# Both score blocks of a tile multiplied before the first read, and PSUM tiles of one bank for the paired products

## The chip, the cores and the metric

The kernel runs on one core of one Trainium2 chip. The metric is the device time of one execution in microseconds, the median of the runs shown. The engines are TensorE (PE; its weight loads are listed apart as PEld), VectorE (DVE), ScalarE (ACT), GpSimd (POOL) and SyncE (SP, which here issues most transfers).

## The reference

One inference step of a hybrid decoder layer, for a prompt of 512 tokens and for 8 decode sequences of 4 tokens (544 token columns in all, width 2048), all in float32:

```python
u = x @ w_in                      # 18952 columns: q, k, v, o, z of the mLSTM; q, k, v, z of attention; two merge gates; i, f
h_m, C, n, m = mlstm(q_m, k_m, v_m, ig, lf, C0, n0, m0)
h_a = sliding-window attention with sinks (32 heads of 64, 4 KV heads, window 128)
br_m = layernorm_per_head(h_m) * norm_w * sigmoid(o_m) * silu(z_m)
br_a = h_a * silu(z_a)
y = sigmoid(g_m) * (br_m @ w_proj_m) + sigmoid(g_a) * (br_a @ w_proj_a)
out = layernorm(alpha * x + y @ w_out) * ln_w + ln_b
```

The prompt's attention goes by blocks of 128 queries; block j sees the keys of blocks j-1 and j:

```python
s = q @ k.T / sqrt(64) - slope * dist       # masked outside the window
p = softmax(concat([s, sink]))[:-1]
out = p @ v
```

Further outputs are the states and the last keys and values of both parts.

## The kernel before

Every float32 product is made of three products of a faster type: the weights are split into a high part `wh` (ScalarE, line 184) and a low part `wl` (VectorE, line 185), the activations likewise, and hi*hi, hi*lo and lo*hi are added up in PSUM.

The work has three stretches. First come x, its transposes and a few plain products for keys, values and gates (to about 87 us). Then the stage of this change, 72 *pairs* (`paired`, lines 627 to 651): a pair takes two column tiles of 128 of `w_in` and computes a 2 x 2 block product (two halves of the inner dimension, two halves of the 544 columns) in seven products in place of eight, with sums of the halves. Last come `w_proj_a`, `w_proj_m` and `w_out` as plain products (from about 1988 us).

A pair runs as seven steps n = 0 to 6. `half_product` (line 582) issues 24 matmuls of 272 columns: 16 with `wh` (line 593), 8 with `wl` (line 595). They go to three sums, called bank 0 (A), 1 (D) and 2 (B), in the order `BANK = [0, 1, 2, 0, 2, 1, 2]`. Products 0, 1 and 2 open a sum, the later ones add to it. After each product `gather` (line 597) reads the sum that was just written:

- n = 0: ScalarE copies A to `p1` (line 604); n = 1: ScalarE copies D (line 612); n = 3: ScalarE copies A (line 617)
- n = 2, 4, 5, 6: VectorE combines B, B, D and B with earlier results (lines 615, 619, 621, 623)

The sums lie in PSUM tiles of two banks from the pool `psA`, which has two buffers: X is allocated at n = 0 and holds A and D in its two banks; Y is allocated at n = 2 and uses only its first bank, for B. The same pool serves the plain products. A second pool, `psB`, has four tiles of one bank (`sm()`) for everything else.

The weights of step n + 2 are split ahead (`prepare`, with a higher priority), into two buffers each for `wh` and `wl`. The weights of the next pair are loaded at n = 3 and n = 4.

Between the steps `tick()` lets other generators issue a piece of their work. One of them, `attentions()`, goes through 16 attentions of two heads each (lines 682 to 745). Its first part makes the scores: for each head and each of four blocks j, two matmuls (`k1`, `k2`, line 700) and one VectorE instruction (line 702) that adds the distance term, clips and keeps the row minimum. Blocks 0 and 1 lie in the two halves of one `sm()` tile, blocks 2 and 3 in those of another. The exponentials follow on ScalarE (line 711), the normalisation (line 717), two steps later the transposes (line 728) and the product with the values (line 738). The attentions take place from about 193 to 1070 us; after them comes the attention of the decode tokens and then, from about 1190 us, their mLSTM part (lines 1042 to 1089).

The order of TensorE's instructions in this stage is that of the program text (`manual_schedule`, line 1183). The other engines' queues are ordered by a planner from priorities; all waits between engines are set from the tiles that an instruction reads and writes.

Of the kernel before, what the change touches and what calls it, by code (L numbers as in the profile page):

```python
# [15 lines left out]
F32 = mybir.dt.float32  # L16
F32R = mybir.dt.float32r
AF = mybir.ActivationFunctionType
ALU = mybir.AluOpType
# [54 lines left out]
def _build(tc, nc, i, o, es):  # L74
    PSUM = bass.MemoryType.PSUM
    ALL = slice(0, 128)

    def pool(stack, name, bufs, space=None, side=None):
        kw = {"space": space} if space is not None else {}
        if space is None:  # L80
            kw["side"] = side or "right"
            kw["reuse_waits"] = "tile"
        return stack.enter_context(tc.tile_pool(name=name, bufs=bufs, **kw))

    y_p, y_s, C_p, n_p, m_p, kb_p, vb_p, C_s, n_s, m_s, kb_s, vb_s = o
    V, A, G, PE = nc.vector, nc.scalar, nc.gpsimd, nc.tensor
# [3 lines left out]
    wr = pool(es, "wr", 3)  # L90
    wp = pool(es, "wp", 2)
    evp = pool(es, "ev", 3)
    psA = pool(es, "psA", 2, PSUM)
    psB = pool(es, "psB", 4, PSUM)
    dr = pool(es, "dr", 1, bass.MemoryType.DRAM)

    count = [0]

    def nm(s):
        count[0] += 1  # L100
        return f"{s}_{count[0]}"

    def sm():
        return psB.tile([128, 512], F32, tag="sm", name=nm("sm"))
# [16 lines left out]
    def spawn(g):  # L121
        live.append(g)
# [8 lines left out]
    def drain():  # L131
        while live:
            tick()
# [10 lines left out]
    nsinkb = cst.tile([128, AH], F32, name="nsinkb")  # L144
# [53 lines left out]
    EVEN = ((0, 0, 272), (1, 272, 272))  # L198

    def mm():  # L200
        return psA.tile([128, 2, 512], F32, tag="mm", name=nm("mm"))

    def gemm(wv, c0, xh, xl, cols=EVEN, raws=(None, None), every=8, prio=0, before=None):
        ps = mm()
# [31 lines left out]
    HT = T // 2  # L236
# [277 lines left out]
    for kk in range(2):  # L514
        ps = gemm(win, VA_ + kk * 128, xh, xl, raws=((raw0[0], raw0[1]), (raw0[2], None))[kk], every=4, prio=150 * kk,
                  before=gates_between if kk else None)
# [63 lines left out]
            add("b21", "b21", "b11")  # L580

    def half_product(w, n):
        bank = BANK[n]
        if n == 0:
            w["X"] = mm()
        if n == 2:
            w["Y"] = mm()
        ps = w["Y"][:, 0, :HT] if bank == 2 else w["X"][:, bank, :HT]
        wh, wl = w.pop(("hl", n))
        x, first = XS[n], n in (0, 1, 2)  # L590
        for k in range(8):
            for p in range(2):
                PE.matmul(ps, wh[:, k], x(p, k), start=(first and k == 0 and p == 0), stop=False, skip_group_check=True)  # L593
        for k in range(8):
            PE.matmul(ps, wl[:, k], x(0, k), start=False, stop=(k == 7), skip_group_check=True)  # L595

    def gather(w, n):

        A0, D0, B0 = w["X"][:, 0, :HT], w["X"][:, 1, :HT], w.get("Y")
        B0 = B0[:, 0, :HT] if B0 is not None else None  # L600
        sc = w["scale"]
        if n == 0:
            w["p1"] = pe_.tile([128, HT], F32, tag="p1", name=nm("p1"))
            A.activation(w["p1"][:], A0, AF.Copy, scale=sc)  # L604
            return
        if n == 1:
            w["O1"], w["O2"] = ev(), ev()
        c11, c21 = (w["O1"][:, c:c + HT] for c in (0, HT))
        c12, c22 = (w["O2"][:, c:c + HT] for c in (0, HT))
        p1 = w["p1"][:]  # L610
        if n == 1:
            A.activation(c11, D0, AF.Copy, scale=sc)  # L612
            G.tensor_tensor(out=c22, in0=p1, in1=c11, op=ALU.subtract)  # L613
        elif n == 2:
            V.scalar_tensor_tensor(c12, B0, sc, p1, op0=ALU.mult, op1=ALU.subtract)
        elif n == 3:
            A.activation(c11, A0, AF.Copy, scale=sc)  # L617
        elif n == 4:
            V.scalar_tensor_tensor(c22, B0, -sc, c22, op0=ALU.mult, op1=ALU.add)
        elif n == 5:  # L620
            V.scalar_tensor_tensor(c12, D0, sc, c12, op0=ALU.mult, op1=ALU.add)
        else:
            V.scalar_tensor_tensor(c21, B0, sc, p1, op0=ALU.mult, op1=ALU.subtract)
# [3 lines left out]
    def paired(work, first=iter(())):  # L627

        steps = [(w, n) for w in work for n in range(7)]
        ready = 0  # L630
        load_a(work[0])
        load_b(work[0])
        for at, (w, n) in enumerate(steps):

            while ready < min(at + 3, len(steps)):
                with tc.high_priority(offset=AHEAD):
                    prepare(*steps[ready])
                ready += 1
            p = at // 7 + 1
            if p < len(work):  # L640
                if n == 3:
                    load_a(work[p])
                elif n == 4:
                    load_b(work[p])
            half_product(w, n)
            with tc.high_priority(offset=AHEAD):
                gather(w, n)
            next(first, None)
            if n == 6:
                w["end"](w["O1"], w["O2"])  # L650
            tick()
# [30 lines left out]
    def attention(k, qs, sz, kv):  # L682


        k1, k2, VA = kv
        hT = btile("b1", [128, SEQ], "hT")
        st = []
        for a in range(2):
            nb = btile("b1", [128, 256], f"nb{a}")
            A.activation(nb[:], cc[:, C_DIST:C_DIST + 256], AF.Copy, scale=SLOPES[2 * k + a])  # L690
            s_ = scores_tile()
            mx, mn, sums = (btile("bm", [128, 4], t_) for t_ in ("mx", "mn", "sums"))
            h = slice(2 * k + a, 2 * k + a + 1)
            for j in range(4):
                if j % 2 == 0:
                    pp = sm()
                w0 = 128 if j == 0 else 0
                c0, k0 = (j % 2) * 256, max(j - 1, 0) * 128
                for n, kx in enumerate((k1, k2)):
                    PE.matmul(pp[:, c0 + w0:c0 + 256], qs[a][:, j * 128:j * 128 + 128], kx[:, k0:k0 + 256 - w0],  # L700
                              start=(n == 0), stop=(n == 1))
                V.tensor_tensor_reduce(s_[:, j, w0:256], pp[:, c0 + w0:c0 + 256], nb[:, w0:256], 1.0, nsinkb[:, h],
                                       ALU.add, ALU.min, accum_out=mn[:, j:j + 1])
            st.append((s_, mx, mn, sums, h))
            yield
        yield
        for a in range(2):
            s_, mx, mn, sums, h = st[a]
            for j in range(4):
                sj = s_[:, j, 128 if j == 0 else 0:256]  # L710
                A.activation(sj, sj, AF.Exp, bias=mn[:, j:j + 1], scale=-1.0, accum_out=sums[:, j:j + 1])
            A.activation(mx[:], mn[:], AF.Exp, bias=sinkb[:, h])
            V.tensor_tensor(out=sums[:], in0=sums[:], in1=mx[:], op=ALU.add)
            V.reciprocal(sums[:], sums[:])
            for j in range(4):
                sj = s_[:, j, 128 if j == 0 else 0:256]
                A.activation(sj, sj, AF.Copy, scale=sums[:, j:j + 1])
            yield
        yield
        for a in range(2):  # L720
            s_ = st[a][0]

            ph, pl = (btile("bt", [128, 7, 128], t_, F32R) for t_ in ("ph", "pl"))
            for m0_, m1_ in ((0, 4), (4, 7)):
                pt = sm()
                for m in range(m0_, m1_):
                    b, own = m // 2, m % 2 == 0
                    PE.transpose(pt[:, (m - m0_) * 128:(m - m0_) * 128 + 128],
                                 s_[:, b, 128:256] if own else s_[:, b + 1, 0:128], ident)
                n = m1_ - m0_  # L730
                hilo(blk(pt[:, 0:n * 128], n), ph[:, m0_:m1_], pl[:, m0_:m1_])
            yield
            yield
            po = sm()
            for b in range(4):
                n = 256 if b < 3 else 128
                for m, p_ in enumerate((ph, pl)):
                    PE.matmul(po[:, b * 128:b * 128 + n], VA[:, b], p_[:, 2 * b:2 * b + n // 128],
                              start=(b == 0 and m == 0), stop=(b == 3 and m == 1), skip_group_check=True)
            rows_ = slice(a * 64, a * 64 + 64)  # L740
            A.copy(hT[rows_], po[64:128])
            V.tensor_tensor(out=hT[rows_], in0=po[0:64], in1=hT[rows_], op=ALU.add)
        yield
        G.tensor_tensor(out=hT[:], in0=sz[:, 0:SEQ], in1=hT[:], op=ALU.mult)
        nc.sync.dma_start(d_bra[k][:, 0:SEQ], hT[:])
# [430 lines left out]
    work += merge_gates[7:]  # L1176
    last = last_sum(s4)
    gates_ = gates(gates_ps)
    spawn(gates_)
    spawn(attentions())  # L1180
    spawn(samples())

    with tc.manual_schedule(engines={PE.engine}):
        paired(work, last)
        drain()

    def branch(src, p, tmp, ahead=()):

# [406 lines left out]
```

## Time and profile before

| | us |
|---|---|
| time, median of 3 runs (2724.84 to 2729.0) | 2725.93 |
| time of the profiled execution | 2723.85 |
| its span, first to last instruction | 2722.0 |
| mean granted TensorE clock | 0.983 |

The profile is of one execution. Its page has the busy time of each engine; further views group the instructions by line (busy time, mean duration, idle time of the engine before them and what ended it), list the waits, give the busy time in chosen stretches with the granted clock, and show the instructions in order of time. A row such as `mm<-s1h,wh` reads: writes the tile `mm`, reads `s1h` and `wh`. The tile `mm` stands for X and Y, `sm` for the one-bank tiles. The operand of the seven products is a11, s1, n2, xk, n3, s4, xk in this order, so that a row tells which product it belongs to.

### The profile page before, as it was taken

To read this page: it belongs to the slowest core of one execution; us is meant where nothing else is said; L and a number is where in the kernel's file an instruction comes from. 1 tells how busy PE (TensorE), PEld (TensorE's weight loads), DVE (VectorE), ACT (ScalarE), POOL (GpSimd) and SP (SyncE) were. 2 spreads that over 40 slices of the span, in tenths; PEclk is the share of its full clock that TensorE was granted. 3 is DMA by queue.
4 is the path that set the end of the run, shared out by engine and by line. 5 is a ranking of instruction groups with operands and counts; after the bars stand their busy time and mean duration, and the time that the engine had idled before them with its cause. 6 is when DMAs were issued, how large, how long until landed. Compare 5 with 4: busy or idle time off the path is not lost.

```text
span 2722.0 us, 48851 instructions
## 1 busy us (share of the span) xinstructions
PE 2575.7 (95%) x19994; PEld 2493.5 (92%) x19994; DVE 1713.2 (63%) x2508; ACT 1188.6 (44%) x1908; POOL 363.7 (13%) x334
## 2 busy tenths in 40 slices
PE   8999988999889989999999999999999999999997
PEld 7998988988888988989989999889999999999997
DVE  7766666666656666657777777777765654333336
ACT  4456566555655565533333343434443333222221
POOL 2111111111111111112111122221000000000002
PEclk9999999999999999989999999999999999999999
DMA  6565555555545555346747666466555546444532
GB/s 188 145 157 130 135 128 127 132 128 139 127 124 142 137 126 139 93 111 211 233 151 238 186 193 211 146 207 215 164 170 183 178 155 198 138 135 149 148 93 90
DMA packets 537103, 421.86 MB, mean 155 GB/s; under 512 B 43536, under 2 KB 449344, under 8 KB 536592
## 3 DMA queue, kind: packets, MB, share of 16 engines
q1 hardware_dynamic: 526800, 382.04, 46.7%
q0 software_dynamic: 10080, 36.70, 7.4%
q8 instruction: 157, 2.57, 0.4%
q14 instruction: 66, 0.54, 0.1%
HBM read 297.66 MB, written 86.42 MB: 141 GB/s over the span
## 4 chain that ended last, share of the span: by engine, by line
PE 51%; DVE 3%; ACT 1%; issue 1%; DMA 0%; POOL 0%; DVEq 0%; SPq 0%; ACTq 0%
PE mm L193 20%; PE mm L593 16%; PE mm L595 7%; PE sm L1258 2%; PE sm L1080 1%; PE sm L1290 1%; PE sm L1074 1%; PE sm L1303 1%; PE sm L193 1%; DVE wl L185 1%; DVE raw L570 0%; ACT wh L184 0%; DVE z L1497 0%; PE sm L1237 0%; PE sm L1313 0%
## 5 line engine op out<-in xcount | busy, mean ns | idle before, releaser
L184 ACT CAST wh<-raw 128x1024 fp32r<-128x1024 f32 x604 | 633.7, 1049 | 1117.8 <-PE mm L593 764.3
L185 DVE TENSOR_TENSOR wl<-raw,wh 128x1024 fp32r<-128x1024 f32 x604 | 749.6, 1242 | 426.4 <-ACT wh L184 406.2
L593 PE MATMUL mm<-xk,wh 128*128 128x272 f32 x2304 | 322.4, 294 | 0.0
L593 PEld LDWEIGHTS mm<-xk,wh 128*128 128x128 f32 x2304 | 307.4, 194 | 2.7 <-ACT wh L184 0.8
L570 DVE TENSOR_TENSOR raw<-raw,raw 128x1024 f32<-128x1024 f32 x218 | 276.8, 1271 | 4.7 <-DMA raw<-in_w_in 1.1
L193 PE MATMUL mm<-bh,wl 128*128 128x272 f32 x1024 | 214.0, 289 | 0.0
L193 PE MATMUL mm<-bh,wh 128*128 128x272 f32 x1024 | 213.6, 290 | 0.0
L193 PE MATMUL mm<-bl,wh 128*128 128x272 f32 x1024 | 213.3, 288 | 0.0
L593 PE MATMUL mm<-s1h,wh 128*128 128x272 f32 x576 | 159.3, 307 | 47.5 <-ACT p L604 47.4
L613 POOL TENSOR_TENSOR ev<-p,ev 128x272 f32<-128x272 f32 x72 | 107.7, 1496 | 518.8 <-ACT ev L612 514.6
L595 PE MATMUL mm<-xk,wl 128*128 128x272 f32 x1152 | 169.9, 290 | 0.0
L593 PEld LDWEIGHTS mm<-s1h,wh 128*128 128x128 f32 x576 | 112.0, 194 | 61.1 <-ACT p L604 60.8
L193 PEld LDWEIGHTS mm<-bh,wh 128*128 128x128 f32 x1024 | 160.7, 188 | 2.3 <-issue 2.3
L193 PEld LDWEIGHTS mm<-bl,wh 128*128 128x128 f32 x1024 | 161.4, 188 | 0.0
L193 PEld LDWEIGHTS mm<-bh,wl 128*128 128x128 f32 x1024 | 160.9, 189 | 0.0
L595 PEld LDWEIGHTS mm<-xk,wl 128*128 128x128 f32 x1152 | 155.8, 191 | 0.0
L593 PE MATMUL mm<-s1l,wh 128*128 128x272 f32 x576 | 152.6, 296 | 0.0
L593 PE MATMUL mm<-n2h,wh 128*128 128x272 f32 x576 | 152.1, 295 | 0.0
L593 PE MATMUL mm<-n2l,wh 128*128 128x272 f32 x576 | 151.6, 295 | 0.0
L593 PE MATMUL mm<-n3h,wh 128*128 128x272 f32 x576 | 150.9, 293 | 0.0
L593 PE MATMUL mm<-n3l,wh 128*128 128x272 f32 x576 | 150.6, 293 | 0.0
L593 PE MATMUL mm<-s4h,wh 128*128 128x272 f32 x576 | 149.0, 290 | 0.3 <-ACT ev L617 0.3
(427 smaller groups left out, 5562.9 us busy)
## 6 DMA issues: line engine op xcount, KB each, us to landing
raw<-in_w_in SPq DMA_DIRECT2D x296, 512.0 KB, 3.9
raw<-raw POOLq DMA_DIRECT2D x70, 512.0 KB, 4.9
C<-in_state_mlstm_C SPq DMA_DIRECT2D x32, 1024.0 KB, 6.1
out<-C SPq DMA_DIRECT2D x64, 512.0 KB, 4.1
raw<-in_w_proj_a SPq DMA_DIRECT2D x32, 512.0 KB, 5.9
raw<-in_w_proj_m SPq DMA_DIRECT2D x32, 512.0 KB, 4.2
raw<-in_w_out SPq DMA_DIRECT2D x32, 512.0 KB, 4.5
d_sgm<-ev SPq DMA_DIRECT2D x16, 272.0 KB, 2.7
```

Of the source, the lines that this page charges most:

```text
L184: A.copy(wh[:], raw[:])
L185: V.tensor_tensor(out=wl[:], in0=raw[:], in1=r32(wh[:]), op=ALU.subtract)
L193: PE.matmul(ps[:, f, :w], a[:, kk], b(k, c, w), start=(k == 0 and n == 0), stop=(k == 15 and n == 2))
L570: V.tensor_tensor(out=w[out][:], in0=w[a][:], in1=w[b][:], op=ALU.add)
L593: PE.matmul(ps, wh[:, k], x(p, k), start=(first and k == 0 and p == 0), stop=False, skip_group_check=True)
L595: PE.matmul(ps, wl[:, k], x(0, k), start=False, stop=(k == 7), skip_group_check=True)
L613: G.tensor_tensor(out=c22, in0=p1, in1=c11, op=ALU.subtract)
L1074: PE.matmul(pC[c * 32:c * 32 + 32, :], qz[:, c], ct[:, c], start=(b == 0), stop=(b == NB - 1), tile_position=(0, c * 32))
L1080: PE.matmul(pu[:], Ab[:, c * 128:c * 128 + 128], r["V4"][:], start=True, stop=True)
L1258: PE.matmul(pp[:, 0:258], a[:, b * 128:b * 128 + 128], b_[:, b, f], start=(b == 0 and n == 0), stop=(b == 3 and n == 2))
L1290: PE.matmul(pp[:, 0:n], x_[c][:, b * 128:b * 128 + 128], y_[c][:, b * 128:SEQ], start=(c == 0 and m == 0), stop=(c == 3 and m == 2))
L1303: PE.matmul(pp[:, 0:258], x_[:, off:off + 128], y_[:, b, f], start=(b == 0 and n == 0), stop=(b == j and n == 2))
```

## The change

Three things change. In the scores, the matmuls of both blocks of a tile are issued first and then the two VectorE reads. In the paired stage, the pool of two tiles of two banks is closed and the same four banks are opened as four tiles of one bank; A, D and B are each a tile of their own, taken at n = 0, 1 and 2, and the pool of two-bank tiles is opened again after the stage. So that the pool can be closed, the first piece of the gates' work, which reads the plain products' last two-bank tile (lines 341 to 346), is issued before the stage and not at its first `tick()`.

```diff
-    psA = pool(es, "psA", 2, PSUM)
     psB = pool(es, "psB", 4, PSUM)
+    esP, psA = es.enter_context(ExitStack()), {}
+
+    def open_psum(pairs):
+
+        esP.close()
+        psA["mm"] = pool(esP, "psP" if pairs else "psA", 4 if pairs else 2, PSUM)
+
+    open_psum(False)
...
     def mm():
-        return psA.tile([128, 2, 512], F32, tag="mm", name=nm("mm"))
+        return psA["mm"].tile([128, 2, 512], F32, tag="mm", name=nm("mm"))
...
     def half_product(w, n):
-        bank = BANK[n]
-        if n == 0:
-            w["X"] = mm()
-        if n == 2:
-            w["Y"] = mm()
-        ps = w["Y"][:, 0, :HT] if bank == 2 else w["X"][:, bank, :HT]
+        if n < 3:
+            w["bank", n] = psA["mm"].tile([128, 512], F32, tag="bank", name=nm("bank"))
+        ps = w["bank", BANK[n]][:, :HT]
...
     def gather(w, n):
 
-        A0, D0, B0 = w["X"][:, 0, :HT], w["X"][:, 1, :HT], w.get("Y")
-        B0 = B0[:, 0, :HT] if B0 is not None else None
+        A0, D0, B0 = (w["bank", b][:, :HT] if ("bank", b) in w else None for b in range(3))
...
-            for j in range(4):
-                if j % 2 == 0:
-                    pp = sm()
-                w0 = 128 if j == 0 else 0
-                c0, k0 = (j % 2) * 256, max(j - 1, 0) * 128
-                for n, kx in enumerate((k1, k2)):
-                    PE.matmul(pp[:, c0 + w0:c0 + 256], qs[a][:, j * 128:j * 128 + 128], kx[:, k0:k0 + 256 - w0],
-                              start=(n == 0), stop=(n == 1))
-                V.tensor_tensor_reduce(s_[:, j, w0:256], pp[:, c0 + w0:c0 + 256], nb[:, w0:256], 1.0, nsinkb[:, h],
-                                       ALU.add, ALU.min, accum_out=mn[:, j:j + 1])
+            for j2 in (0, 2):
+                pp = sm()
+                w0s = [128 if j == 0 else 0 for j in (j2, j2 + 1)]
+                for j, w0 in zip((j2, j2 + 1), w0s):
+                    c0, k0 = (j % 2) * 256, max(j - 1, 0) * 128
+                    for n, kx in enumerate((k1, k2)):
+                        PE.matmul(pp[:, c0 + w0:c0 + 256], qs[a][:, j * 128:j * 128 + 128], kx[:, k0:k0 + 256 - w0],
+                                  start=(n == 0), stop=(n == 1))
+                for j, w0 in zip((j2, j2 + 1), w0s):
+                    c0 = (j % 2) * 256
+                    V.tensor_tensor_reduce(s_[:, j, w0:256], pp[:, c0 + w0:c0 + 256], nb[:, w0:256], 1.0, nsinkb[:, h],
+                                           ALU.add, ALU.min, accum_out=mn[:, j:j + 1])
...
     gates_ = gates(gates_ps)
+    next(gates_)
     spawn(gates_)
...
     with tc.manual_schedule(engines={PE.engine}):
+        open_psum(True)
         paired(work, last)
         drain()
+    open_psum(False)
```

## The prediction

> **What bounds the kernel now.** I read the page first, then the stage windows, the waits of TensorE, the timeline at the two waits, and last the rows of the engines that feed TensorE. Columns of a windows row: stretch and length, busy us (x instructions) of PE, PEld, DVE, ACT, POOL, then granted clock, DMA share, GB/s.
>
> ```profile
> span 2722.0 us, 48851 instructions
> PE 2575.7 (95%) x19994; PEld 2493.5 (92%) x19994; DVE 1713.2 (63%) x2508; ACT 1188.6 (44%) x1908; POOL 363.7 (13%) x334
> ```
> ```profile
> 87.00:193.00 106.00, 98.20 (x762) 96.48 (x761) 69.97 (x100) 51.09 (x68) 14.59 (x17) 0.98 0.61 149
> 193.00:1040.00 847.00, 760.75 (x5814) 745.10 (x5813) 532.33 (x856) 508.67 (x930) 126.81 (x106) 0.97 0.54 131
> 1200.00:1700.00 500.00, 492.20 (x3767) 457.48 (x3766) 380.74 (x456) 191.79 (x238) 110.01 (x104) 1.00 0.64 199
> 2010.00:2500.00 490.00, 490.00 (x3883) 485.17 (x3883) 234.93 (x458) 144.09 (x228) 8.79 (x16) 1.00 0.50 156
> ```
>
> TensorE bounds everywhere. It is full from 2010 on and nearly full from 1200 to 1700; the place with air is 193 to 1040, where the attention runs between the products: 86 us of 847 idle, and the only long stretch with a clock of 0.97. What ends that idle time, over the whole run (us in total, times, longest):
>
> ```profile
> PE sm L700 <- DVE mn L702: 62.9, 64, 2.8
> PE mm L593 <- ACT p L604: 47.4, 47, 4.1
> PE sm L1038 <- ACT w L925: 4.8, 2, 3.9
> ...
> PE mm L593 <- DVE ev L621: 0.6, 1, 0.6
> ...
> PE mm L593 <- ACT ev L617: 0.3, 1, 0.3
> ```
> ```profile
> PEld sm L700 <- DVE mn L702: 74.2, 64, 2.9
> PEld mm L593 <- ACT p L604: 60.8, 53, 4.4
> ```
>
> Two waits carry nearly all. The first is in the scores, the second at the second product of a pair (operand s1). The page's groups say that only this product waits, while its neighbours show none:
>
> ```profile
> L593 PE MATMUL mm<-s1h,wh 128*128 128x272 f32 x576 | 159.3, 307 | 47.5 <-ACT p L604 47.4
> ...
> L593 PE MATMUL mm<-n2h,wh 128*128 128x272 f32 x576 | 152.1, 295 | 0.0
> ```
>
> **The scores.** One attention, engine by engine (start, us, engine, line; idle before in brackets):
>
> ```profile
> 305.68 0.33 PE L700 MATMUL sm<-k,q 128*128 128x128 f32 x2
> 305.88 0.44 DVE L615 SCALAR_TENSOR_TENSOR ev<-mm,p 128x272 f32<-128x272 f32 x1 [2.53 <-PE mm L595]
> 306.23 1.22 DVE L185 TENSOR_TENSOR wl<-raw,wh 128x1024 fp32r<-128x1024 f32 x1
> 307.37 0.34 DVE L702 CUSTOM_DVE_ANT_0 s<-sm,nb,nsinkb 128x128 f32<-128x128 f32 x1
> ...
> 307.77 0.74 PE L700 MATMUL sm<-k,q 128*128 128x256 f32 x4 [1.77 <-DVE mn L702]
> ...
> 309.27 0.50 PE L700 MATMUL sm<-k,q 128*128 128x256 f32 x2 [0.75 <-DVE mn L702]
> ```
>
> TensorE multiplies block 0, then stands until VectorE has read it, because block 1 goes into the same tile; VectorE comes to that read only after a gather and a split (0.44 and 1.22). Blocks 1 and 2 then run together (x4: block 2 opens another tile), and block 3 waits for the read of block 2. That is two waits for each head, 2 heads x 16 attentions x 2 = 64, the count of the row. The change multiplies both blocks of a tile before the first read, so TensorE's order has no read between two writes of a tile, and all 64 go. Worth: a matmul's row ends later than the next one could start. Eight matmuls of the row of 626.79 below take 1.16 us and the last of them 0.29, so they start 0.124 apart, and each idle time counts 0.29 - 0.124 = 0.16 us too little. 62.9 + 64 x 0.16 = 73.1 us; the weight loads' row gives 74.2. I take 73, with 63 and 74 as ends.
>
> Added: VectorE's first read now waits for two more matmuls, about 2 x 0.13 us, then reads two blocks in a row. Behind it on VectorE stand splits and gathers, and ScalarE's exponentials wait for it. The transposes of these scores, two steps later, show no idle time (row of L728 below), so 64 x 0.26 = 17 us of later reads lie under the products; on the path they would make the gain 17 us less. The Trainium skill, "PSUM — Partial Sum Buffer", section "PSUM bank collisions raise a hardware error", says that a write and a read by two engines must not meet in one bank and quadrant, whichever columns they touch, while different banks run clean; the rows agree that block 1 waits for a read of other columns, and by that rule the later first read cannot be avoided.
>
> **The pair's products.** Second product of a pair:
>
> ```profile
> 626.79 1.16 PE L595 MATMUL mm<-a11h,wl 128*128 128x272 f32 x8
> ...
> 627.74 1.33 ACT L763 ACTIVATE q<-ev 64x544 fp32r<-64x544 f32 x2 [1.33 <-DVE ev L623]
> ...
> 629.10 1.04 ACT L184 CAST wh<-raw 128x1024 fp32r<-128x1024 f32 x1
> 630.17 0.40 ACT L604 ACTIVATE p<-mm 128x272 f32<-128x272 f32 x1
> ...
> 630.62 0.40 PE L593 MATMUL mm<-s1h,wh 128*128 128x272 f32 x1 [2.67 <-ACT p L604]
> ```
>
> It writes bank 1 of tile X and waits for ScalarE's read of bank 0, which stands behind 1.33 and 1.04 us of other ScalarE work. So the two banks count as one, and the waits for L617 and L621 (X again, at the sixth product and the next pair's first) are of the same kind. With a tile for each bank the read of A is in the way only of the fourth product, two products (some 6 us) later; D needs the second product's read, also ScalarE's; B (three products, VectorE) stays as it was, with one product between read and next write. Four tiles for three banks mean that a pair's A takes a free one, D the former A and B the former D, all read at least two products before. Worth: 47.4 + 47 x 0.16 = 54.9, ends 47 and 61; L617 and L621 add 0.9 + 0.3 = 1.2.
>
> **The clock.** Around another scores wait, in stretches of 3.41 us, and matmuls of the third and fourth:
>
> ```profile
> 297.38:300.79 3.41, 1.75 (x13) 1.40 (x11) 2.30 (x7) 3.38 (x7) 2.05 (x2) 1.00 0.00 0
> 300.79:304.21 3.42, 3.42 (x15) 3.42 (x16) 0.83 (x4) 2.54 (x11) 0.58 (x1) 0.50 0.70 134
> ```
> ```profile
> 301.38 0.43 PE L593 MATMUL mm<-n2h,wh 128*128 128x272 f32 x1
> 301.61 0.43 PE L593 MATMUL mm<-n2l,wh 128*128 128x272 f32 x1
> ...
> 304.42 0.28 PE L593 MATMUL mm<-n2h,wh 128*128 128x272 f32 x1
> 304.54 0.29 PE L593 MATMUL mm<-n2l,wh 128*128 128x272 f32 x1
> ```
>
> A stretch in which TensorE was busy for 1.75 of 3.41 us is followed by one at half the clock, in which the same matmul starts every 0.23 us and not every 0.12. The stage row's 0.97 over 847 us says that 25 us of full clock are missing there, and the row from 87 another 2. From 1200 to 1700, where only the products' shorter waits are left, the clock is 1.00. So the drop is a consequence of the waits; without them I expect nearly all back. Part of the missing clock fell on time in which TensorE stood anyway (4 or 5 us): I take 22, ends 0 and 27.
>
> **What it costs, and what is late next.** Product 0 of the first pair starts in a pool that opens only when the former tiles are read, and the stage's last pool closes after the last gather:
>
> ```profile
> 87.01 0.29 PE L593 MATMUL mm<-a11h,wh 128*128 128x272 f32 x1
> ...
> 87.96 0.60 ACT L528 COPY ev<-mm 128x544 f32<-128x544 f32 x1
> ...
> 1986.94 0.43 DVE L623 SCALAR_TENSOR_TENSOR ev<-mm,p 128x272 f32<-128x272 f32 x1
> ...
> 1988.13 0.50 PE L193 MATMUL mm<-bh,wh 128*128 128x272 f32 x2
> ```
>
> The keys' copy ends at 88.56, so product 0, and all of TensorE's queue behind it, may stand 1.6 us, once. At the end the gather is over at 1987.37, before the first large product at 1988.13: nothing; the transposes between are the cover, and without them it is under half a microsecond. The gates' reads only move ahead of the first product.
>
> Next could be late the splits (high part on ScalarE, low part on VectorE), the gathers, the transposes. For the window 193 to 1040 and, in the third row, for the whole run:
>
> ```profile
> L184 ACT CAST wh<-raw 128x1024 fp32r<-128x1024 f32 x213 | 223.3, 1048 | 247.6 <-PE mm L593 238.3 <-DMA raw<-in_w_in 3.9 <-ACT nb L690 3.0
> L185 DVE TENSOR_TENSOR wl<-raw,wh 128x1024 fp32r<-128x1024 f32 x213 | 266.7, 1252 | 114.1 <-ACT wh L184 101.4 <-ACT s L717 7.3 <-PE mm L595 3.1
> ...
> L728 PE MATMUL sm<-cc,s 128*128 128x128 f32 x224 | 30.1, 274 | 0.0
> ```
>
> ScalarE stands 238 us of this stage waiting for TensorE to give back a weight buffer. The stage would shrink by 73 + 25 (its part of the 55 by length, 847 of the 1899 us from 87 to 1986 that the pairs take) + 22 = 120, so ScalarE would be busy 509 of 727 us, 70%, and VectorE 532, 73%. From 1200 to 1700 VectorE is 76% busy and TensorE waits for hardly anything. Some bursts will still be late: I allow 5 us, ends 0 and 20 (20 is one wait of 1.1 us, the scores' mean, in some 18 of the 32 heads).
>
> **Sum.** Against the profiled execution (2723.85 us, span 2722.0): 73 + 55 + 1 + 22 - 1.6 - 5 = 144.4 gained, so about 2579. The median of three runs is 2725.93, 2.1 above it: I predict 2581. The ends of the forecast itself: 74 + 61 + 1 + 27 = 163 gained, about 2563; 63 + 47 + 10 (under half of the clock's 22) - 1.6 - 20 = 98, about 2628; that all terms end on one side together is not likely.
>
> **Rivals.**
> The clock does not come back (0.08): the half-rate stretches have another cause, such as a limit on a full array. Then the 22 us stay and the time is 2603. Against it stands the row from 2010 to 2500: 490 of 490 us busy at 1.00. The Trainium skill, "TensorE: Matmul & The Clock Gate", section "What's actually happening", puts the fall to half rate after a whole idle window of about 3.4 us; by it, waits of 1 to 3 us would cost no clock and this term would be zero. The row disagrees: the stretch before the drop was half busy.
>
> ScalarE or VectorE becomes the bound in the attention stage (0.08): no row shows ScalarE at 70% beside a full TensorE. If VectorE could not pass 70% there, the stage would last 532 / 0.70 = 760 instead of 727, and the time would be 2614. For it: bursts of exponentials stand in one queue with the splits. Against it: the 238 us of waiting for TensorE above.
>
> The products' wait stays (0.04), because ScalarE's count or a reused bank still ties the second product to the read: 2581 + 55 = 2636. That neither wait goes (0.02) would leave 2726.
>
> Slower (0.03): the loads of a pair, issued in the fourth and fifth step of the pair before, have some 24 us in place of 28 (213 splits are 30 pairs) and share SyncE's queue with stores that wait for their data. If the first split of each pair then waited for its load, the 30 pairs of the attention stage decide it at 144 / 30 = 4.8 us each; at 5.5 us the time is 2746. Against it:
>
> ```profile
> ACT wh L184 <- DMA raw<-in_w_in: 12.5, 4, 8.0
> ```
>
> Four splits of the whole run waited, and from 1200 to 1700 the transfers ran at 0.64 and 199 GB/s, above what the attention stage would need (131 x 847 / 727 = 153).
>
> **The numbers.** The forecast has 0.75. A difference under 0.2% (5.4 us) can hardly be told from no change here. Faster by more: 0.75 + 0.08 + 0.08 + 0.04 = 0.95; the same 0.02; slower 0.03. The range runs from 2560, just under the forecast's best sum, to 2620, which takes in the clock and the supply rivals and most of the forecast's bad end.
>
> **What would show it.** In the changed profile the waits of the score matmuls for L702's read and of the second product for L604 should be gone from the list, not merely shorter; TensorE from the first product to the attention's end should take some 120 us less, with a clock of 0.99 or 1.00; the stage from 1200 should shrink only by the products' waits, about 20 us; from the first large product after the pairs on nothing should change. The forecast is wrong if a new wait of 20 us or more stands in the list (for wh, wl or a gather), if the clock stays near 0.97, or if ScalarE stops waiting for TensorE.

## The result, and the profile after

| | before | after |
|---|---|---|
| median, us | 2725.39 (4 runs, 2724.59 to 2729.0) | 2569.65 (4 runs, 2563.45 to 2570.61) |
| profiled execution, us | 2723.85 | 2563.45 |
| its span, us | 2722.0 | 2561.7 |
| mean granted clock | 0.983 | 0.993 |

The ratio is 0.9421, with a 95% interval of 0.9404 to 0.9439: 155.7 us less by the medians, 160.4 between the two profiled executions. The forecast was 144 less, to 2581.

The head of the page after, then stretches that answer to those of before (the attention stretch is now 190 to 902; the row of before ran 9 us past the last score matmul, so lengths compare by the starts given below), and the waits of TensorE down to 1.3 us:

```profile
span 2561.7 us, 48818 instructions
PE 2524.2 (99%) x19994; PEld 2464.3 (96%) x19994; DVE 1707.2 (67%) x2508; ACT 1173.2 (46%) x1908; POOL 362.3 (14%) x334
```
```profile
190.00:902.00 712.00, 711.95 (x5741) 711.74 (x5740) 519.60 (x842) 485.88 (x909) 122.86 (x105) 1.00 0.64 154
902.00:1060.00 158.00, 154.16 (x1315) 149.07 (x1314) 109.55 (x152) 77.71 (x138) 21.18 (x18) 0.98 0.48 128
1060.00:1560.00 500.00, 498.82 (x3852) 468.11 (x3852) 388.84 (x467) 196.30 (x245) 112.81 (x105) 1.00 0.66 203
1870.00:2360.00 490.00, 490.00 (x3893) 485.69 (x3893) 230.65 (x445) 142.74 (x224) 8.80 (x16) 1.00 0.51 161
```
```profile
PE sm L1043 <- ACT w L930: 5.1, 2, 3.9
PE sm L969 <- POOL rep L964: 3.8, 1, 3.8
PE sm L277 <- DMA cc<-in_consts: 2.7, 1, 2.7
PE mm L200 <- ACT ev L529: 2.4, 1, 2.4
PE bank L597 <- ACT wh L191: 1.9, 1, 1.9
PE sm L472 <- ACT ev L535: 1.4, 1, 1.4
PE bank L597 <- DVE ev L622: 1.3, 1, 1.3
PE mm L200 <- DVE wl L192: 1.3, 1, 1.3
```

Lines have moved: products are 597 and 599, score matmuls 703, the split's high part 191, its low part 192. In the tables of waits, the three figures are us in total, times and longest. Both large waits are gone from the list. TensorE is busy for 711.95 of 712 us of the attention stretch, at full clock. The eight matmuls of a head's scores run as one row:

```profile
192.01 1.10 PE L703 MATMUL sm<-k,q 128*128 128x128 f32 x8
195.97 1.10 PE L703 MATMUL sm<-k,q 128*128 128x128 f32 x8
```

By the matmuls' starts, the time from the first product to the last score matmul fell from 943.6 to 813.1 us (130.5 less), from there to the decode tokens' preparation from 166.9 to 155.5 (11.4), from there to the last product (its last matmul with `wh`) from 787.0 to 766.9 (20.1). What follows took 737.4 and takes 737.3. The first product starts 1.7 us later.

### The profile page after: what moved, and what is told of

The parts are those of the page before. It is cut to its first block, busy times and chain, and to the rows that moved or that the text cites. A ratio compares the mean times of both kernels' runs of the same rounds, so it can differ in the third digit from the quotient of the medians.

```text
span 2561.7 us, 48818 instructions
## 1 busy us (share of the span) xinstructions
PE 2524.2 (99%) x19994; PEld 2464.3 (96%) x19994; DVE 1707.2 (67%) x2508; ACT 1173.2 (46%) x1908; POOL 362.3 (14%) x334
## 4 chain that ended last, share of the span: by engine, by line
PE 57%; DVE 1%; issue 0%; POOL 0%; ACT 0%; DVEq 0%
PE mm L200 21%; PE bank L597 17%; PE bank L599 9%; PE sm L1266 2%; PE sm L1085 1%; PE sm L1079 1%; PE sm L1298 1%; PE sm L1311 1%; PE sm L200 1%; DVE z L1505 0%; PE sm L1245 0%; PE sm L1321 0%; PE sm L1253 0%; DVE z L1510 0%; PE sm L1448 0%
## 5 line engine op out<-in xcount | busy, mean ns | idle before, releaser
L597 PE MATMUL bank<-xk,wh 128*128 128x272 f32 x2304 | 312.7, 288 | 1.3 <-DVE ev L622 1.3
L597 PEld LDWEIGHTS bank<-xk,wh 128*128 128x128 f32 x2304 | 297.7, 188 | 4.2 <-ACT wh L191 2.4
L599 PE MATMUL bank<-xk,wl 128*128 128x272 f32 x1152 | 168.1, 288 | 0.0
L599 PEld LDWEIGHTS bank<-xk,wl 128*128 128x128 f32 x1152 | 153.4, 189 | 0.0
L597 PE MATMUL bank<-n2h,wh 128*128 128x272 f32 x576 | 149.1, 290 | 1.9 <-ACT wh L191 1.9
L597 PE MATMUL bank<-s1h,wh 128*128 128x272 f32 x576 | 150.5, 292 | 0.0
L597 PE MATMUL bank<-s1l,wh 128*128 128x272 f32 x576 | 149.3, 292 | 0.0
L597 PE MATMUL bank<-s4h,wh 128*128 128x272 f32 x576 | 149.0, 290 | 0.0
L597 PE MATMUL bank<-a11h,wh 128*128 128x272 f32 x576 | 148.7, 290 | 0.0
L597 PE MATMUL bank<-n2l,wh 128*128 128x272 f32 x576 | 148.7, 291 | 0.0
```

## The experiments

Changes against "before" stand as ratios with their intervals. The two parts first, each alone.

**The scores alone.** The kernel before, with this part of the change and nothing else of it:

```diff
-            for j in range(4):
-                if j % 2 == 0:
-                    pp = sm()
...
+            for j2 in (0, 2):
+                pp = sm()
...
```

> The scores of the change alone; the paired products keep their tiles of two banks. Theory (two separate waits, each worth its idle time, and the clock follows the idle time): the 64 waits of the score matmuls are gone, the second product still waits for L604 about 50 times and 47 to 61 us; gain about 73 us of waits, some 7 us of slow first matmuls after a wait and 15 to 20 us of clock, so about 2630 us. Rival (the waits stand in for each other, TensorE only arrives sooner at the next late engine): the waits at the second product grow to over 80 us and the time is above 2665.

Measured: 2640.75 us, ratio 0.9685 (0.9669 to 0.9702), 85 us less. The score waits are gone; the other stays and has grown a little (47.4 before):

```profile
PE mm L593 <- ACT p L604: 51.2, 47, 4.1
```

The time is 10 us above the value expected and well below the rival's bound. Some 4 us of the 10 are this wait's growth and 3 the clock behind the attention (37.5 us at half rate up to the last product, 31.3 before).

**The one-bank tiles alone.** The changed kernel, with the scores put back:

```diff
-            for j2 in (0, 2):
-                pp = sm()
...
+            for j in range(4):
+                if j % 2 == 0:
+                    pp = sm()
...
```

> The one-bank tiles of the change alone; the scores are multiplied and read block by block as before. Theory: the waits for L604 are gone, the 64 waits of the scores stay at about 63 us of PE idle time, half-rate stretches remain in the attention stage because two scores waits lie in one stretch of 3.4 us; gain 55 us plus some 10, so about 2662 us. Rival (they stand in for each other): the scores' waits grow by 20 us or more and the time is above 2690.

Measured: 2658.14 us, ratio 0.9759 (0.9733 to 0.9785), 67 us less. The wait for L604 is gone and the scores' waits are what they were:

```profile
PE sm L703 <- DVE mn L705: 61.9, 64, 2.8
```

So neither wait stands in for the other. The parts give 3.15 and 2.41%, together 5.56; the change gives 5.79. The remainder is within the intervals, but the clock shows where it would come from. The time in which the trace records half the clock, between the first product and the last score matmul, is 47.2 us before, 17.1 with the scores alone, 44.4 with the tiles alone and nothing with both.

**D and B in one tile.** This asks whether the two banks of a tile count as one. It is the kernel of the scores alone, with two-bank tiles that are shared in another way (the gathers read accordingly):

```diff
         if n == 0:
-            w["X"] = mm()
-        if n == 2:
             w["Y"] = mm()
-        ps = w["Y"][:, 0, :HT] if bank == 2 else w["X"][:, bank, :HT]
+        if n == 1:
+            w["X"] = mm()
+        ps = w["Y"][:, 0, :HT] if bank == 0 else w["X"][:, bank - 1, :HT]
...
```

> The scores of the change, two-bank tiles, but D and B share the tile X and A lies alone in Y. Theory (the two banks of a tile count as one, so a product waits for the read that was issued right before it in the other bank): the wait for L604 is gone and three others come for each pair, at the third product for ScalarE's read of D (L612), at the sixth for VectorE's read of B (L619), at the seventh for VectorE's read of D (L621), 216 in all at 0.6 to 1 us: some 120 us more than with the scores alone, about 2750 us. Rival (the banks are apart and the second product waits for a count or an order of ScalarE's queue): no such waits, the time is that of the scores alone or less.

Measured: 2713.49 us, ratio 0.9957 (0.994 to 0.9973), 73 us above the scores alone. Its waits:

```profile
PE mm L593 <- DVE ev L621: 52.5, 63, 2.6
PE mm L593 <- ACT ev L612: 29.6, 46, 2.6
PE mm L593 <- DVE ev L619: 19.3, 31, 1.3
PE mm L593 <- ACT s L719: 7.6, 11, 0.7
```

The wait for L604 is gone and the three foretold ones are there, at the three products that now follow a read of their tile's other bank. That settles the cause: in this kernel a tile of two banks counts as one in the waits. It is a matter of how the waits are set; in the changed kernel ScalarE reads A from 92.57 to 92.96 while TensorE, from 92.45 on, writes D into another bank.

The 11 waits for L719, the scores' normalisation, are put down wrongly, for it reads no PSUM. All stand at the sixth product and end 0.146 us after VectorE's read of B, as most of those for L619 do. With them, 151 of the 216 places wait as foretold. The size, 73 us for 120, was too high: where TensorE does not wait, work of another generator lies between the two products.

**Three tiles in place of four.**

```diff
-        psA["mm"] = pool(esP, "psP" if pairs else "psA", 4 if pairs else 2, PSUM)
+        psA["mm"] = pool(esP, "psP" if pairs else "psA", 3 if pairs else 2, PSUM)
```

> The changed kernel with three one-bank tiles in the pool of the pairs and not four. Theory (what counts is that A, D and B are tiles of their own): every bank is read two products or more before the next pair writes it, so no new wait and the changed kernel's time, within 8 us. Rival (the fourth tile carries part of the gain): a wait at the first or third product of a pair for the last read of the pair before (L622 or L626), 30 us or more.

> The changed kernel once more, beside the three below. Every theory: about 2568 us.

Measured: 2565.91 us, ratio 0.941 (0.9393 to 0.9426); the changed kernel beside it 2569.10, ratio 0.9421 (0.9405 to 0.9437). No difference: the separate tiles count, the fourth bank carries nothing.

**A tile for each block of the scores, in the old order.** The kernel of the one-bank tiles alone, and in its scores:

```diff
-                if j % 2 == 0:
-                    pp = sm()
+                pp = sm()
```

> The changed kernel with the scores in the old order (multiply a block, read it), but each block in a tile of its own. Theory (the wait was for the bank that is being read, not for the order of issue): no waits of the score matmuls for the reads, the changed kernel's time within 10 us. Rival (the read must be issued after both blocks, or the four tiles of the second pool are now short): 30 us or more above it, with waits of the score matmuls.

Measured: 2567.31 us, ratio 0.9414 (0.9396 to 0.9433), and no wait of the score matmuls. The order of issue is only one way out; a write that goes to another tile, and so to another bank, than the read is as good.

**The clock.** In the tiles-alone kernel, matmuls that nobody reads fill the waits:

```diff
+                if j % 2 == 0:
+                    junk = sm()
+                    for _ in range(5):
+                        PE.matmul(junk[:, 0:256], qs[a][:, 0:128], k1[:, 0:256], start=True, stop=True)
                 V.tensor_tensor_reduce(s_[:, j, w0:256], pp[:, c0 + w0:c0 + 256], nb[:, w0:256], 1.0, nsinkb[:, h],
```

> The one-bank tiles of the change, scores block by block as before, and five matmuls of 256 columns into a spare tile after blocks 0 and 2 of each head, whose result nobody reads. The wait for the read stays, but TensorE works through most of it. Theory (a half idle stretch of 3.4 us costs the clock in the next one): the half-rate stretches in the attention stage go, the clock there is 0.99 or 1.00, and the time is 10 to 20 us below that of the one-bank tiles alone although there is more work. Rival (the clock has another cause, or only a wholly empty stretch lowers it): clock unchanged at 0.97, time the same or up to 15 us above.

Measured: 2636.52 us, ratio 0.9673 (0.9656 to 0.969), 22 us below the tiles alone, with 320 matmuls more. The attention stretch, first of the tiles alone, then with the waits filled:

```profile
190.00:997.00 807.00, 745.07 (x5734) 733.94 (x5733) 527.18 (x848) 501.75 (x918) 125.44 (x105) 0.97 0.57 136
```
```profile
190.00:975.00 785.00, 765.12 (x6077) 755.17 (x6076) 527.85 (x849) 502.19 (x919) 126.53 (x107) 1.00 0.59 140
```

The reads came nearly as late as before (those of blocks 0 and 2 ended 1.18 us after the block's first matmul in the mean, 1.27 without the filling), and the clock came back. 44.4 us at half rate became none: 22 us of full clock, the whole gain. So the idle time itself cost the clock, though in the tiles-alone kernel the emptiest stretch of 3.41 us before a drop still had 0.6 us of work, and most had half. From the first product to the last score matmul, the traces of before and of the tiles alone have 22 drops. One follows a stretch that was wholly idle; the others follow stretches with 1.59 to 2.80 us idle. No full-clock stretch there with less than 1.59 us idle was followed by one; from 1.59 to 1.67 some were and some were not. The rule of the Trainium skill weighed in the prediction ("TensorE: Matmul & The Clock Gate", "What's actually happening": a fall to half rate after an idle window) does not hold here as it is put there, since 21 of these 22 drops came without a wholly idle stretch; the same page's section "A second HAM failure mode: psum-queue depth-cycling" says that frequent short idle times make the clock swing, and with that the runs agree.

**What is left.** Two waits of about 4 us stand in the list after, and at the end of each a half-rate stretch of 6.8 us begins.

```diff
         G.tensor_copy(rep[:], ks_[:].unsqueeze(2).to_broadcast([128, 4, 4, NS]))
         yield
+        yield
+        yield
...
-        for _ in range(3):
+        for _ in range(5):
             yield
         pt = sm()
```

> The changed kernel, with two more steps of products between GpSimd's copy and the matmuls that read it in the decode tokens' preparation, and two more before the transposes that wait for ScalarE's normalisation. Theory (what is left of TensorE's idle time in the pairs are those two waits of about 4 us, with a half-rate stretch of 6.8 us behind each): both waits gone, 10 to 14 us below the changed kernel. Rival (they move with the other engines' queues): same time.

Measured: 2553.19 us, ratio 0.9369 (0.9352 to 0.9385), 16 below the changed kernel measured beside it, where 10 to 14 were expected. Both waits are gone. The decode chain now ends beside the last product, and the first large product waits for the pool that opens again:

```profile
1818.94 0.49 PE L200 MATMUL mm<-bh,wh 128*128 128x272 f32 x2 [2.02 <-DVE ev L626]
```

That is the cover named in the prediction (the transposes between the last gather and the first large product). Without it the price was put at under half a microsecond; it is 2.0.

**Half rate without a wait.** The repeated run of the changed kernel spent 18.3 us at half rate between the attention and the decode preparation, the first one 4.8. The stretch before such a drop, the one after, and the whole part:

```profile
1009.00:1012.40 3.40, 3.40 (x31) 2.80 (x29) 3.40 (x5) 1.05 (x1) 0.00 (x0) 1.00 0.00 0
1012.40:1015.80 3.40, 3.40 (x19) 2.96 (x19) 0.83 (x3) 0.80 (x3) 0.00 (x0) 0.50 0.53 143
```
```profile
902.00:1060.00 158.00, 157.95 (x1309) 152.72 (x1308) 107.16 (x150) 76.61 (x138) 17.34 (x14) 0.95 0.44 118
```

TensorE is shown busy for all of the first stretch. It held matmuls of 32 columns (the decode tokens' values). The profile of before has the same three times, 3.40 of 3.40 us busy from 1154.1, 1164.4 and 1178.0 and half the clock behind each. Such a matmul starts about 0.115 us after the one before it, hardly sooner than one of 272 columns (0.125); as the ends of the rows are modelled, part of the array's time may have been empty in these stretches too. Spread out:

```diff
                 PE.matmul(dst, vas[:, kvh * 64:kvh * 64 + 64], PT[:32, 128 + kvh * 32:160 + kvh * 32], start=False, stop=True, tile_position=tp)
+                if kvh % 2 and not (b % 2 and kvh == 3):
+                    yield
```

> The changed kernel, with the small matmuls of the decode tokens' value product (32 columns each) issued in portions of 8 instructions in place of 32 between two products of the pairs; same work. Theory (matmuls of 32 columns count as little activity, so a stretch of 3.4 us full of them costs the clock in the next one although TensorE is shown as busy): the half-rate stretches between the attention's end and the decode preparation go, all but the one behind the wait for L964, some 12 to 17 us at half rate less than in the repeated run of the changed kernel, 6 to 9 us less time, about 2561 us. Rival (the drop has another cause, such as the transposes or ScalarE): the stretches stay and the time is the changed kernel's.

Measured: 2561.60 us, ratio 0.9393 (0.938 to 0.9406), about 8 below the changed kernel. The same part:

```profile
902.00:1060.00 158.00, 157.99 (x1353) 153.10 (x1352) 112.14 (x148) 80.81 (x142) 18.86 (x13) 1.00 0.47 125
```

The clock of this part went from 0.95 to 1.00, and the four executions have mean clocks of 0.994 to 0.996 where the eight of the changed kernel have 0.990 to 0.993. That the time came out at the value expected is in part luck. With longer chains the preparation now starts later, so that the two waits for L930 also shrank (from 5.1 to 1.9 us) and the half-rate stretch of 6.8 us behind the longer one went, some 6 us together; against that stand new waits, such as 1.2 us for a load behind the last product. What the spreading is worth is read from the clock of its part.

**Both together.** The two lines above, and later steps in two places only:

```diff
-        yield
+        for _ in range(1 if h else 3):
+            yield
...
-        for _ in range(3):
+        for _ in range(5 if h == 2 else 3):
             yield
```

> The portions of the run above, and the later steps only where the changed kernel waits long: two more before the first head's preparation matmuls, two more before the third head's transposes, so that the decode chain still ends before the last pair. Theory: no half-rate stretch left in the pairs, both waits of 4 us gone, 18 to 24 us below the changed kernel, about 2547 us. Rival (the longer chain runs past the last pair and is paid there, as with the later steps everywhere): 2555 us or more.

Measured: 2552.21 us, ratio 0.9359 (0.9346 to 0.9372), some 17 below the changed kernel and the lowest median here, but 5 above the value expected. Both long waits are gone (a short one of 1.2 us is left), and so is the half rate behind the attention; one half-rate stretch of 3.4 us stays at 117 us. Where the rest of the 5 us lies was not found. Against the later steps alone the intervals overlap.

## Why the prediction was right, point by point

**The scores' waits (73).** Gone, all 64. That the later first read costs nothing held: the transposes show no wait. That it cannot be avoided was too strong: with a tile for each block the first read need not wait for the second block, and the time is the same.

**The products' waits (55).** Gone. Their place was read roughly: the prediction gave 25 us of them to the attention stretch by its length, but 24 of the 47 waits and 34 us lay there, since the waits there are longer. This is one reason why that stretch lost 130.5 us where some 120 were forecast. From the preparation on, where they were nearly the only waits that the change could take, 20.1 us came out, where about 20 were forecast. That the two banks counted as one is shown by the run with D and B together; that three tiles would do as well was not seen beforehand.

**The clock (22).** In the attention stretch 47.2 us at half rate fell to none: 23.6 us, shown to be the waits' doing by the filled waits. The clock in the decode tokens' part was not in the sum. In the first profile it happened to be good (4.8 us at half rate where 17.7 were before), in the repeated one not (18.3). That is 6 or 7 us, and most likely why the profiled executions differ by 160 and the medians by 156: the other three executions of the changed kernel have mean clocks of 0.990 and 0.991 where the profiled one has 0.993.

**What was missing.** A wait costs more than its idle time. After the wait that ended at 630.62 the next matmuls start so:

```profile
630.85 0.29 PE L593 MATMUL mm<-s1l,wh 128*128 128x272 f32 x1
630.98 0.29 PE L593 MATMUL mm<-s1h,wh 128*128 128x272 f32 x1
```

From the start of the first matmul to the next it is 0.23 us, from there on 0.13. Over 44 such waits at full clock this first distance is 0.234 in the mean, against 0.125 for the same product without a wait; over 54 waits of the scores it is 0.223, where neighbours take 0.12. What causes it was not tested. At some 0.1 us, the 64 + 47 waits cost 11 us. That is as much as lies between the 144 forecast and the 156 measured, but other terms were off by a few us as well, so the match is not a proof. In the groups after, the second product has lost it (307 ns before):

```profile
L597 PE MATMUL bank<-s1h,wh 128*128 128x272 f32 x576 | 150.5, 292 | 0.0
```

The terms of the attention stretch (waits 73 + 34, first matmuls 9, clock 24, less 4 of new waits and 2 of clock that fell on idle time) give 134, where 130.5 were measured; 3 or 4 us stay unassigned.

**The costs.** Forecast 1.6 at the start: 1.7. The wait does not stand at product 0 but at the keys' transposes (L472), which now come before it in TensorE's queue and wait for the same copy. New waits, forecast 5: 1.9 for a split and 1.3 for a gather. The end of the stage: nothing, as forecast, while its cover lasts.

**The rivals.** ScalarE and VectorE did not bind: 485.88 and 519.60 of 712 us, 68 and 73% (forecast 70 and 73), beside a TensorE that never stands. Their reserve was read rightly from ScalarE's wait for TensorE, 238.3 us before; now (190 to 902):

```profile
L191 ACT CAST wh<-raw 128x1024 fp32r<-128x1024 f32 x210 | 219.4, 1045 | 142.3 <-PE bank L597 118.2 <-ACT s L716 12.6 <-ACT ph L231 7.0
```

It shrank by 120 us, nearly what the stretch lost: the time taken from TensorE's waits was taken from ScalarE's. The loads did not become late: in this stage TensorE waits for none, and no split on ScalarE does either (before, two did, 3.9 us). Two splits wait 4.1 us for a sum of weights that is made by a DMA (`raw<-raw`), which does not reach TensorE.

## What to carry to other kernels

When the bound engine waits in a pattern, look at what the waiting write and the read have in common: here it was a tile of two banks, and tiles cut to what one read needs took the wait away, with three as well as with four. Price a wait of TensorE at its idle time, plus about 0.1 us for the first matmul, plus the clock where idle times add up to about half of a stretch of 3.41 us (here 1.59 us or more). Before counting on it, read from the other engines how long they wait for the bound one; that is the reserve out of which the gain comes.

## What the runs showed of the hardware

After a wait, the second matmul starts about twice as long after the first as it does without one (0.234 against 0.125 us at full clock). Most stretches of 3.41 us with 1.59 to 2.80 us idle were followed by half the clock, and filling the idle time with matmuls took 44.4 us at half rate to none. And a stretch in which TensorE is shown busy for 3.40 of 3.40 us, with matmuls of 32 columns, was followed by half rate three times in the profile of before and three times in the repeated run of the changed kernel; with the same matmuls in smaller portions between large ones the clock stayed at 1.00. Whether the columns, the rows or the pauses between such small matmuls decide was not tried.
